# Ranking a router's experts on the chip, and giving the three smallest ranks 64 token slots instead of 96

## The chip, the cores and the metric

The kernel runs on one core of one Trainium2 chip. Its time is the device time of one execution in microseconds (us), and the time that counts is the median of the runs shown. A profiled execution of the same kernel, with a span from the first to the last instruction, is where all rows below come from.

## The reference

A decoder trunk of two layers runs on 256 tokens of width 1024 in float32. The change touches only the last stage, the expert layer of the second layer:

```python
logits = (h @ w_router + b_router).astype(jnp.float32)
top_val, top_idx = lax.top_k(logits, TOP_K)          # TOP_K = 2 of N_EXPERTS = 8
top_w = jax.nn.softmax(top_val, axis=-1)
...
for e in range(N_EXPERTS):
    out = out + gates[..., e:e + 1] * swiglu(h, wg[e], wu[e], wd[e])
```

Each token goes to two experts of eight, so there are 512 pairs of token and expert. An expert has three weight matrices of 1024 by 3584 in float32, which is 44.04 MB; the eight have 352.3 MB. With the inputs used here the reference's router gives experts 0 to 7 56, 59, 48, 73, 67, 64, 63 and 82 tokens.

## The kernel before

After attention, the recurrent mixer and the dense layer, `moe` runs the router and then the experts 0 to 7 one after the other. For each expert a one-hot matrix of token slots (`oh`, 96 slots) gathers the tokens into `g` with matmuls (`gather`), and a second one-hot matrix with the gates in it (`ohT`, made in `way_back`) brings the results back (`scatter`).

The array of TensorE is used with the tokens as the stationary operand, 32 slots at a time, and the weights as the moving one. Four such matmuls, on four groups of 32 columns of the array, take four different stretches of a weight tile. 96 slots are TG = 3 such groups of tokens, so each weight tile is streamed through TensorE three times. An expert's hidden width is cut into two parts (`PARTS`): part 0 has 16 tiles of 1 MB for gate and up (`up`, L1355) and 8 tiles of 1 MB for down (`down`, L1389), part 1 has 16 tiles of 0.75 MB and 6 of 1 MB. So an expert has 46 weight tiles. The order on TensorE is up of (expert, part), then down of the part before it, transposes of the hidden values (`hidden`), after part 0 `gather` and `way_back` of the next expert, and after the down of part 1 `scatter`.

The weight tiles come in this order of use through a ring of 15 buffers of 1 MB (`rawt` 3, `rawy` 1, `raw` 5, `rawx` 6). SyncE (SP) issues every load (L1203). It takes them in program order, so that a load waits until the tile that had its buffer 15 tiles earlier has been used, and all later loads wait behind it.

When more than 96 tokens fall on one expert, `over` is above zero and a branch at the end runs all experts again for the tokens left out. `noi`, `no` and `Go` count them. On TensorE the one matmul for that count (`pn`, L1470) stands ahead of the first `up`.

Of the kernel before, what the change touches and what calls it, by code (L numbers as in the profile page):

```python
# [21 lines left out]
P = 128  # L22
# [83 lines left out]
def tile_trunk(ctx: ExitStack, tc: tile.TileContext, a, out, fo, mo):  # L106
# [1049 lines left out]
    def moe(l, mix):  # L1156
# [6 lines left out]
        PARTS = ((0, 512), (4 * 512, 384))  # L1163
        TG, CAP = 3, 96

        def sources():

            def ups(e, s):
                c0, n = PARTS[s]
                for nm in ("w_exp_gate", "w_exp_up"):  # L1170
                    for k in range(KD):
                        yield a[nm][0, e, k * P:(k + 1) * P, c0:c0 + 4 * n].rearrange("(k p) n -> p k n", p=P)

            def downs(e, s):
                c0, n = PARTS[s]
                for r0 in range(c0, c0 + 4 * n, 2 * P):
                    yield a["w_exp_down"][0, e, r0:r0 + 2 * P, :].rearrange("(k p) n -> p k n", p=P)
# [138 lines left out]
        def gather(e):  # L1316

            oh = ep.tile([P, 2, CAP], F32, name="oh", tag="oh", bufs=1)
            for i in range(2):
                sel_ = nc.vector.tensor_scalar(oh[:, i, :], C["iota"][:, :CAP], slot_of[:, i, e:e + 1], None, op0=OP.is_equal)  # L1320
            g = gs[e] = ep.tile([P, KD, CAP], F32, name="g", tag="g", bufs=2)
            for k0 in range(0, KD, 4):
                ps = bank()[:, :4 * CAP].rearrange("p (k n) -> p k n", k=4)
                for k in range(4):
                    ks = slice((k0 + k) * P, (k0 + k + 1) * P)
                    for i in range(2):
                        nc.tensor.matmul(ps[:, k, :], xn[:, i, ks], oh[:, i, :], start=i == 0, stop=i == 1)
                for k in range(4):
                    c = k0 + k
                    affine(k0 // 4, g[:, c, :], ps[:, k, :], am[:, c:c + 1], sh[:, c:c + 1])  # L1330
            return sel_

        def way_back(e):

            ohT = st[e] = ep.tile([P, TG, S], F32, name="ohT", tag="ohT", bufs=2)
            pt = [bank("pt").rearrange("p (t n) -> p t n", t=2) for _ in range(2)]
            for i in range(2):
                oh = ep.tile([P, TG, 4, 32], F32, name="ohg", tag="ohg", bufs=2)
                nc.vector.tensor_scalar(oh, C["iota"][:, :CAP].rearrange("p (t n) -> p t n", t=TG)[:, :, None, :].to_broadcast([P, TG, 4, 32]),
                                        slot_of[:, i, e:e + 1], G[:, i, e:e + 1], op0=OP.is_equal, op1=OP.mult)  # L1340
# [3 lines left out]
            nc.vector.tensor_copy(ohT[:, 2, :], pt[1][:, 0, :])  # L1344
# [15 lines left out]
        def product_of(s, pss):  # L1360
            n, out = PARTS[s][1], []
            for t in range(TG):
# [6 lines left out]
        def hidden(s, sgs):  # L1369
# [3 lines left out]
            for t in range(TG):  # L1373
# [6 lines left out]
        def down(s, hid, acc):  # L1380

            nb = PARTS[s][1] // P
            for m in range(4 * nb):
# [3 lines left out]
                for t in range(TG):  # L1387
# [4 lines left out]
        def scatter(e, acc):  # L1392
            ohT, end = st.pop(e), e == NE - 1
            y = ep.tile([P, TG, 256], F32, name="y", tag="y", bufs=1)
            if end:
                nc.vector.tensor_tensor(y[:, 0:2, :], acc[0], gq[0][:, None, :].to_broadcast([P, 2, 256]), op=OP.mult)
                nc.vector.tensor_tensor(y[:, 2, :], acc[1], gq[0], op=OP.mult)
            else:
                nc.scalar.copy(y[:, 0:2, :], acc[0])
                nc.vector.tensor_copy(y[:, 2, :], acc[1])  # L1400
# [3 lines left out]
            for ts in ([0], [1]) if end else ([0, 1],):  # L1404
                sc = [bank("sc")[:, :256 * len(ts)].rearrange("p (i n) -> p i n", i=len(ts)) for _ in range(4)]
                for i in ts:
                    for t in range(TG):
                        for q in range(4):
                            r = slice(32 * q, 32 * q + 32)
                            nc.tensor.matmul(sc[q][:, i - ts[0], :], ohT[r, t, i * P:(i + 1) * P], y[r, t, :],  # L1410
                                             start=t == 0 and i == ts[0], stop=t == TG - 1, skip_group_check=True)
# [45 lines left out]
        gates, gf, gq, y = [], [], [], []  # L1457
        after = gather(0)
        G, t8 = small("G"), small("t8")
# [4 lines left out]
        Go = small("Go")  # L1464
        behind(nc.vector.tensor_scalar(Go, slot_of, float(CAP) + 0.5, None, op0=OP.is_ge), after)
# [8 lines left out]
        def accumulators():  # L1474
            both, one = bank("acc").rearrange("p (t n) -> p t n", t=2), psp.tile([P, 256], F32, name="acc2", tag="ada", bufs=1)
            return (both, one), [both[:, 0, :], both[:, 1, :], one]

        accs, prev = None, None
        for e, s in [(e, s) for e in range(NE) for s in range(2)] + [(None, None)]:
# [4 lines left out]
            if prev:  # L1484
                pe, ps_, hid = prev
                if ps_ == 0:
                    accs = accumulators()
                down(ps_, hid, accs[1])
# [118 lines left out]
```

## Time and profile before

| | |
|---|---|
| median of 3 runs | 1632.04 us (1624.58 to 1632.18) |
| profiled execution, its own time | 1637.66 us |
| its span | 1635.8 us |
| TensorE busy (PE) | 1559.9 us, 95% |
| TensorE weight loads (PEld) | 965.8 us, 59% |
| VectorE (DVE), ScalarE (ACT), GpSimd (POOL) | 569.0, 350.8 and 139.9 us |
| read from HBM | 472.92 MB |

PE is TensorE's matmuls, PEld its loads of stationary operands, DVE VectorE, ACT ScalarE, POOL GpSimd, SPq SyncE's queue of instructions. In a row of a timeline, a bracket gives the idle time just before and what ended it. A float32 matmul of the program is two MATMUL records in the trace, so that the 192 of an `up` are 384 records.

### The profile page before, as it was taken

The numbers are of one execution on the slowest core, as the hardware profiler recorded it, in microseconds if no ns is written. First come the engines' busy times: TensorE is split into PE (matmuls) and PEld (weight loads), VectorE is DVE, ScalarE is ACT, GpSimd is POOL, SyncE is SP. The second block draws the span as 40 slices with busy tenths as digits, with TensorE's granted clock in tenths as the row PEclk, the third lists the DMA queues.
The fourth block names the chain that finished last, engine by engine and source line by source line (L and its number), as shares of the span: only waits on it lengthen the run. The fifth ranks groups of instructions, "written<-read, shape, count | busy, mean of one in ns | idle before, by whom it ended". The sixth has DMA issues, their size and how long they took to land. (4 is left out here: it accounts for less than half of the span.)

```text
span 1635.8 us, 40608 instructions
## 1 busy us (share of the span) xinstructions
PE 1559.9 (95%) x18452; PEld 965.8 (59%) x18452; DVE 569.0 (35%) x1076; ACT 350.8 (21%) x721; POOL 139.9 (9%) x188
## 2 busy tenths in 40 slices
PE   5988999999898999999999999999999999999996
PEld 1976779999797678545355354354354454444444
DVE  2699777755569867310020010010010020110101
ACT  2723335444472323210010010010010010000001
POOL 1225100000145211000000000000000000000010
PEclk9999998999999799999999999999999999999998
DMA  9746347745463555789979979989979989989890
GB/s 319 252 169 226 136 138 274 257 169 176 141 198 130 212 178 200 290 270 415 414 291 417 414 294 417 414 294 418 411 296 417 404 302 417 393 318 416 349 378 31
DMA packets 114604, 476.65 MB, mean 291 GB/s; under 512 B 14735, under 2 KB 23707, under 8 KB 91900
## 3 DMA queue, kind: packets, MB, share of 16 engines
q1 hardware_dynamic: 111932, 469.96, 75.3%
q0 software_dynamic: 2496, 4.05, 0.9%
q8 instruction: 146, 2.39, 0.6%
q14 instruction: 30, 0.25, 0.0%
HBM read 472.92 MB, written 1.05 MB: 290 GB/s over the span
## 5 line engine op out<-in xcount | busy, mean ns | idle before, releaser
L1355 PE MATMUL up<-rawx,g 128*32 128x512 f32 (+1 forms) x2424 | 233.3, 542 | 0.0
L1365 DVE TENSOR_TENSOR sg<-sg,up 128x512 f32<-128x512 f32 (+1 forms) x48 | 29.8, 621 | 541.3 <-PE up L1355 539.8
L1355 PE MATMUL up<-raw,g 128*32 128x384 f32 (+1 forms) x2040 | 194.8, 536 | 0.0
L1355 PEld LDWEIGHTS up<-rawx,g 128*32 128x32 f32 x2424 | 78.3, 110 | 148.4 <-issue 145.2
L1355 PEld LDWEIGHTS up<-raw,g 128*32 128x32 f32 x2040 | 65.2, 110 | 125.0 <-issue 115.6
L1355 PE MATMUL up<-rawt,g 128*32 128x512 f32 (+1 forms) x1272 | 124.0, 540 | 0.0
L1389 PE MATMUL acc<-rawx,hid 128*32 128x256 f32 x2064 | 113.6, 379 | 0.0
L189 DVE TENSOR_TENSOR wlo<-raw,whi 128x512 fp32r<-128x512 f32 x140 | 96.9, 730 | 31.2 <-PE ps L169 18.1
L1389 PE MATMUL acc<-raw,hid 128*32 128x256 f32 x1872 | 103.2, 379 | 0.0
L1389 PEld LDWEIGHTS acc<-rawx,hid 128*32 128x32 f32 x2064 | 67.1, 110 | 46.2 <-issue 2.8
L187 ACT CAST whi<-raw 128x512 fp32r<-128x512 f32 x140 | 80.2, 623 | 58.9 <-PE ps L169 27.9
L169 PE MATMUL ps<-hh,whi 128*128 128x256 f32 x352 | 88.3, 288 | 1.8 <-ACT hh L187 1.8
L169 PE MATMUL ps<-hl,whi 128*128 128x256 f32 x352 | 88.3, 288 | 0.1
L169 PE MATMUL pp<-hh,whi 128*128 128x256 f32 x296 | 80.3, 306 | 6.3 <-ACT hh L187 3.7
L1355 PEld LDWEIGHTS up<-rawt,g 128*32 128x32 f32 x1272 | 40.7, 110 | 77.1 <-issue 69.5
L1389 PEld LDWEIGHTS acc<-raw,hid 128*32 128x32 f32 x1872 | 60.8, 110 | 41.2 <-PE up L1355 1.0
L1364 ACT ACTIVATE sg<-up 128x512 f32<-128x512 f32 (+1 forms) x48 | 26.1, 544 | 263.0 <-PE up L1355 263.0
L1428 POOL TENSOR_TENSOR fa<-fa,gate 128x512 f32<-128x512 f32 x4 | 5.1, 1281 | 886.1 <-ACT gate L272 886.1
L1377 ACT COPY hid<-pt 128x512 f32<-128x512 f32 (+1 forms) x32 | 17.0, 532 | 295.5 <-PE pt L1376 294.5
L169 PE MATMUL pp<-hl,whi 128*128 128x256 f32 x296 | 77.0, 294 | 0.5 <-DVE hl L189 0.2
L244 DVE SCALAR_TENSOR_TENSOR raw<-raw,ccol 128x1024 f32<-128x1024 f32 x56 | 75.0, 1359 | 0.1
L169 PEld LDWEIGHTS ps<-hh,whi 128*128 128x128 f32 x352 | 68.9, 196 | 3.7 <-ACT hh L187 2.2
(431 smaller groups left out, 2246.2 us busy)
## 6 DMA issues: line engine op xcount, KB each, us to landing
rawx<-in_w_exp_down_dram SPq DMA_DIRECT2D x43, 1024.0 KB, 11.4
raw<-in_w_ada_dram SPq DMA_DIRECT2D x40, 1024.0 KB, 6.0
raw<-in_w_exp_down_dram SPq DMA_DIRECT2D x39, 1024.0 KB, 9.9
rawx<-in_w_exp_up_dram SPq DMA_DIRECT2D x38, 1024.0 KB, 15.8
rawt<-in_w_exp_gate_dram SPq DMA_DIRECT2D x23, 1024.0 KB, 14.2
raw<-in_w_exp_gate_dram SPq DMA_DIRECT2D x30, 768.0 KB, 12.2
rawt<-in_w_exp_down_dram SPq DMA_DIRECT2D x22, 1024.0 KB, 14.3
raw<-in_w_exp_up_dram SPq DMA_DIRECT2D x21, 1024.0 KB, 16.3
```

Source lines behind the costliest of these rows:

```text
L169: nc.tensor.matmul(ps, w if left else x, x if left else w, start=start, stop=stop)
L187: c = nc.scalar.copy(hi, src)
L189: v = nc.vector.tensor_sub(lo, src, hi.bitcast(F32))
L244: nc.vector.scalar_tensor_tensor(acc[:, gs], raw[:, gs], ccol[:, k:k + 1], acc[:, gs], op0=OP.mult, op1=OP.add)
L1355: nc.tensor.matmul(ps[t][32 * j:32 * j + 32, :n], g[:, k, 32 * t:32 * t + 32], raw[:, j * n:(j + 1) * n], start=k == 0, stop=k == KD - 1)
L1364: nc.scalar.activation(sg, pss[0][t][:, :n], AF.Silu)
L1365: nc.vector.tensor_mul(sg, sg, pss[1][t][:, :n])
L1377: (nc.vector.tensor_copy if t == 1 else nc.scalar.copy)(hid[:, t, :nb].rearrange("p b n -> p (b n)"), pt[:, :nb * P])
L1389: nc.tensor.matmul(acc[t][32 * q:32 * q + 32, :], hid[:, t, b, 32 * j:32 * j + 32], raw[:, m % 2, 256 * q:256 * q + 256], start=s == 0 and ...
L1428: nc.gpsimd.tensor_mul(fa[:, i, cs], fa[:, i, cs], gates[n])
```

## The change

The number of tokens of each expert is computed on the chip (`pc`), and the experts are ranked by it: expert 0 always has rank 0, the others are ranks 1 to 7 from the most tokens to the fewest. The program takes the ranks in the fixed order 0, 1, 5, 2, 3, 6, 4, 7. Ranks 0 to 4 have 96 slots as before (three groups of 32), ranks 5, 6 and 7 have 64 (two groups): gather, up, transposes, down and scatter of these run for two groups. The weights' addresses of all but the first expert come from registers of SyncE, loaded from `num`. The slots and gates are put in the order of ranks with masks (`slotr`, `Gr`), and the count of tokens that find no slot uses 64 or 96 by rank. The rest of the kernel is as it was; `downs`, `way_back`, `product_of`, `hidden`, `scatter` and `accumulators` get the number of groups in the same way as the functions shown.

```diff
+        RANKS = (0, 1, 5, 2, 3, 6, 4, 7)
+        BIG = 4
+        groups = [3 if r <= BIG else 2 for r in RANKS]
         TG, CAP = 3, 96
+        which = [0]
         def sources():
+            def at(e):
+                return bass.ds(which[e], 1) if e else slice(0, 1)
...
-                        yield a[nm][0, e, k * P:(k + 1) * P, c0:c0 + 4 * n].rearrange("(k p) n -> p k n", p=P)
+                        yield a[nm][0, at(e), k * P:(k + 1) * P, c0:c0 + 4 * n].rearrange("o (k p) n -> p (o k) n", p=P)
...
         def gather(e):
-            oh = ep.tile([P, 2, CAP], F32, name="oh", tag="oh", bufs=1)
+            cap, r, slots = 32 * groups[e], RANKS[e], (ranked if e else by)[0]
+            oh = ep.tile([P, 2, CAP], F32, name="oh", tag="oh", bufs=1)[:, :, :cap]
...
         def up(e, s):
-            n, g, pss = PARTS[s][1], gs[e], []
+            n, g, pss, T = PARTS[s][1], gs[e], [], groups[e]
             for w in range(2):
-                ps = [bank("up") for _ in range(TG)]
+                ps = [bank("up") for _ in range(T)]
                 for k in range(KD):
                     raw = load()[:, 0]
-                    for t in range(TG):
+                    for t in range(T):
...
-        def down(s, hid, acc):
+        def down(s, hid, acc, T):
...
-                for t in range(TG):
+                for t in range(T):
...
         gates, gf, gq, y = [], [], [], []
+        G, t8 = small("G"), small("t8")
+        by, ranked = (slot_of, G), (small("slotr"), small("Gr"))
         after = gather(0)
...
-        Go = small("Go")
-        behind(nc.vector.tensor_scalar(Go, slot_of, float(CAP) + 0.5, None, op0=OP.is_ge), after)
+        pc = bank("pl")[:, :NE]
+        for i in range(2):
+            nc.tensor.matmul(pc, ones, sel[:, i, :], start=i == 0, stop=i == 1)
+        row = lambda t: t[:, None, :].to_broadcast([P, NE, NE])
+        col = lambda t: t[:, :, None].to_broadcast([P, NE, NE])
+        key, rank = ep.tile([P, NE], F32, name="key"), ep.tile([P, NE], F32, name="rank")
+        behind(nc.vector.tensor_scalar(rank, C["iota8"], -float(NE), 1.0e5, op0=OP.is_equal, op1=OP.mult), after)
+        nc.vector.scalar_tensor_tensor(key, pc, float(NE), C["iota8"], op0=OP.mult, op1=OP.subtract)
+        nc.vector.tensor_add(key, key, rank)
+        M, t64 = ep.tile([P, NE, NE], F32, name="M"), ep.tile([P, 2, NE, NE], F32, name="t64")
+        nc.vector.tensor_tensor(M, row(key), col(key), op=OP.is_gt)
+        nc.vector.tensor_reduce(rank, M, axis=AX.X, op=OP.add)
+
+        nc.vector.scalar_tensor_tensor(M, row(rank), -float(NE), col(C["iota8"]), op0=OP.add, op1=OP.is_equal)
+        nc.vector.tensor_tensor(t64[:, 0], M, row(C["iota8"]), op=OP.mult)
+        nc.vector.tensor_reduce(key, t64[:, 0], axis=AX.X, op=OP.add)
+        num = ep.tile([P, NE], I32, name="num")
+        nc.vector.tensor_scalar(num, key, float(NE), None, op0=OP.add)
+        _, nums = nc.values_load_multi_w_load_instructions(num[0:1, :], [mybir.EngineType.SP], min_val=0, max_val=NE - 1)
+        which += [nums[r] for r in RANKS[1:]]
+        for of, to in zip(by, ranked):
+            for i in range(2):
+                nc.vector.tensor_tensor(t64[:, i], M, row(of[:, i, :]), op=OP.mult)
+            nc.vector.tensor_reduce(to, t64, axis=AX.X, op=OP.add)
+
+        Go, caps = small("Go"), ep.tile([P, NE], F32, name="caps")
+        nc.vector.tensor_scalar(caps, rank, BIG + 0.5, 32.0, op0=OP.is_lt, op1=OP.mult)
+        nc.vector.scalar_tensor_tensor(Go, slot_of, -64.5, caps[:, None, :].to_broadcast([P, 2, NE]), op0=OP.add, op1=OP.is_ge)
         no = ep.tile([P, 1], F32, name="no")
         nc.vector.tensor_reduce(no, Go.rearrange("p i e -> p (i e)"), axis=AX.X, op=OP.add)
```


The first place is the start of the expert stage on TensorE. Before, from the last matmul of the slots (`pl`) to the first `up`; L1470 is the count of tokens without a slot:

```order
L1302 MATMUL pl<-sel,cf 128x8
L1303 MATMUL pl<-sel,cf 128x8
L1304 MATMUL pl<-sel,cf 128x8
L1327 MATMUL ps<-oh,xn 128x96 x16
L1470 MATMUL pl<-no,cf 128x1
L1355 MATMUL up<-rawt,g 32x512 x36
```

and now, where L1482 is `pc` and L1512 is that same count:

```order
L1312 MATMUL pl<-sel,cf 128x8
L1313 MATMUL pl<-sel,cf 128x8
L1314 MATMUL pl<-sel,cf 128x8
L1338 MATMUL ps<-oh,xn 128x96 x16
L1482 MATMUL pl<-sel,cf 128x8 x2
L1512 MATMUL pl<-no,cf 128x1
L1368 MATMUL up<-rawt,g 32x512 x36
```

`pc` has come in, and the count still stands ahead of the first `up`; it reads `no`, which VectorE makes.

On VectorE, what stands around the sum `no` for that count before (it is the L1467 row):

```order
L1465 TENSOR_SCALAR Go<-slot 128x16
L1462 TENSOR_TENSOR G<-G,t_7499 128x16 [waits DVE_49]
L1467 TENSOR_REDUCE no<-Go 128x1 [waits DVE_49]
L1339 TENSOR_SCALAR ohg<-cf,slot,G 128x384 [waits DVE_49]
L1468 TENSOR_TENSOR Go<-Go,G 128x16 [waits DVE_49]
L1339 TENSOR_SCALAR ohg<-cf,slot,G 128x384
L366 TENSOR_SCALAR g<-ps,am,modT_91 128x96 [waits PE_49]
L366 TENSOR_SCALAR g<-ps,am,modT_91 128x96 x3
```

and now, from the second row of the ranking on (the `g` rows and the first ranking row, L1487, which reads `pc`, stand just ahead; `no` is the L1509 row, `num` the L1497 row):

```order
L1488 TENSOR_TENSOR key<-key,rank 128x8 [waits DVE_49]
L1490 TENSOR_TENSOR M<-key 128x64 [waits DVE_49]
L1491 TENSOR_REDUCE rank<-M 128x8 [waits DVE_49]
L1493 SCALAR_TENSOR_TENSOR M<-rank,cf 128x64 [waits DVE_49]
L1506 TENSOR_SCALAR caps<-rank 128x8
L1494 TENSOR_TENSOR t_7514<-M,cf 128x64 [waits DVE_49]
L1502 TENSOR_TENSOR t_7514<-M,slot 128x64
L1495 TENSOR_REDUCE key<-t_7514 128x8 [waits DVE_49]
L1507 SCALAR_TENSOR_TENSOR Go<-slot,caps 128x16
L1497 TENSOR_SCALAR num<-key 128x8 [waits DVE_49]
L1502 TENSOR_TENSOR t_7514<-M,slot 128x64
L1509 TENSOR_REDUCE no<-Go 128x1 [waits DVE_49]
```

`no` stood ahead of the first `g`; now it stands behind `g` and behind the ranking, with `num` two rows ahead of it.

The second place is SyncE at the same time. Before, loads of the first expert's weights, the last of `up` in part 0 and the first of `gate` in part 1:

```order
L1203 DMA raw<-in_w_exp_up_dram 128x2048
L1203 DMA rawx<-in_w_exp_up_dram 128x2048 x6
L1203 DMA rawt<-in_w_exp_up_dram 128x2048
L1203 DMA rawt<-in_w_exp_gate_dram 128x1536 x2
L1203 DMA rawy<-in_w_exp_gate_dram 128x1536
```

and now:

```order
L1213 DMA raw<-in_w_exp_up_dram 128x2048
L1213 DMA rawx<-in_w_exp_up_dram 128x2048 x2
L1498 TENSOR_LOAD num
L1498 ISA x16
L1213 DMA rawx<-in_w_exp_up_dram 128x2048 x4
L1213 DMA rawt<-in_w_exp_up_dram 128x2048
L1213 DMA rawt<-in_w_exp_gate_dram 128x1536 x2
```

The load of the eight numbers into registers, and 16 register instructions on them, stand ahead of the last four of the six `rawx` loads. From the next expert on, a register instruction also stands ahead of each load.

The third place is TensorE in the first expert with 64 slots, its part 0. Before (an expert with 96 slots at the same place):

```order
L1376 MATMUL pt<-cf,sg 128x128 x9
L1355 MATMUL up<-rawx,g 32x512 x48
L1355 MATMUL up<-rawt,g 32x512 x36
L1355 MATMUL up<-rawy,g 32x512 x12
L1355 MATMUL up<-raw,g 32x512 x60
L1355 MATMUL up<-rawx,g 32x512 x36
L1389 MATMUL acc<-rawx,hid 32x256 x8
L1389 MATMUL acc_9020<-rawx,hid 32x256 x4
```

and now:

```order
L1389 MATMUL pt<-cf,sg 128x128 x9
L1368 MATMUL up<-rawx,g 32x512 x32
L1368 MATMUL up<-rawt,g 32x512 x24
L1368 MATMUL up<-rawy,g 32x512 x8
L1368 MATMUL up<-raw,g 32x512 x40
L1368 MATMUL up<-rawx,g 32x512 x24
L1402 MATMUL acc<-rawx,hid 32x256 x8
L1402 MATMUL acc_9116<-rawx,hid 32x256 x4
```

Each weight tile has 8 matmuls where it had 12; the down rows that follow are of the expert before, with 96 slots.

## Rows read from the trace of the kernel before

**Rows 1.** Page, the span in 40 slices (40.9 us each).

```profile
DMA  9746347745463555789979979989979989989890
GB/s 319 252 169 226 136 138 274 257 169 176 141 198 130 212 178 200 290 270 415 414 291 417 414 294 417 414 294 418 411 296 417 404 302 417 393 318 416 349 378 31
```

**Rows 2.** Windows: engines' busy time, TensorE clock, DMA share, GB/s, over one expert.

```profile
core 0: us, PE busy (x) PEld busy (x) DVE busy (x) ACT busy (x) POOL busy (x), PEclk, DMA share, GB/s
934.00:1051.00 117.00, 117.00 (x1539) 54.84 (x1535) 11.05 (x22) 7.96 (x16) 0.00 (x0) 1.00 0.94 373
```

**Rows 3.** SyncE's waits, 700 to 1600 us: total us, times, longest.

```profile
SPq L1203 <- PE up L1355: 519.8, 246, 10.3
```

**Rows 4.** Timeline of TensorE over one expert's period: start us, us, what.

```profile
961.52 2.33 PE L1355 MATMUL up<-rawy,g 128*32 128x384 f32 x24
...
1014.66 7.93 PE L1355 MATMUL up<-rawx,g 128*32 128x512 f32 x72
...
1055.88 5.36 PE L1389 MATMUL acc<-rawx,hid 128*32 128x256 f32 x96
...
1072.90 3.71 PE L1327 MATMUL ps<-oh,xn 128*128 128x96 f32 x32
...
1077.20 2.87 PE L1410 MATMUL sc<-y,ohT 32*128 32x256 f32 x48
1080.00 5.23 PE L1355 MATMUL up<-raw,g 128*32 128x384 f32 x60
```

**Rows 5.** Windows inside the expert stage, columns as in rows 2.

```profile
685.00:720.00 35.00, 35.00 (x330) 11.45 (x319) 2.73 (x5) 2.55 (x5) 0.00 (x0) 1.00 0.95 315
...
760.00:785.00 25.00, 25.00 (x389) 12.95 (x381) 0.56 (x1) 0.96 (x2) 0.00 (x0) 1.00 1.01 416
785.00:810.00 25.00, 25.00 (x240) 7.62 (x236) 0.00 (x0) 1.79 (x3) 0.00 (x0) 1.00 1.02 413
...
840.00:846.00 6.00, 6.00 (x87) 3.48 (x89) 4.12 (x8) 1.68 (x5) 0.00 (x0) 1.00 0.01 3
```

**Rows 6.** Timeline of TensorE at the stage's start.

```profile
676.86 0.31 PE L1470 MATMUL pl<-no,cf 128*128 128x1 f32 x2
677.10 7.93 PE L1355 MATMUL up<-rawt,g 128*32 128x512 f32 x72
```

**Rows 7.** Timeline of VectorE at the stage's start.

```profile
664.48 0.26 DVE L1258 TENSOR_REDUCE ws<-wams 128x8 f32<-128x64 f32 x1
...
673.57 0.16 DVE L1467 TENSOR_REDUCE no<-Go 128x1 f32<-128x16 f32 x1
...
675.28 1.24 DVE L366 TENSOR_SCALAR g<-ps,am,modT 128x96 f32<-128x96 f32 x4 [0.25 <-PE ps L1327]
```

**Rows 8.** Timelines of SyncE (its DMA issues), at the stage's start and later.

```profile
662.69 3.27 SPq L1203 DMA_DIRECT2D rawx<-in_w_exp_up_dram  x6
...
845.44 0.33 SPq L1203 DMA_DIRECT2D rawt<-in_w_exp_up_dram  x1
```

**Rows 9.** SyncE's instructions by line: count, ns min/median/max, first and last start.

```profile
L1501 SPq TENSOR_LOAD <-noi x1: 485/485/485, 835.1 to 835.1; - x1
L1501 SPq FUSED_REGOPS  x1: 186/186/186, 835.6 to 835.6; - x1
...
L1203 SPq DMA_DIRECT2D raw<-in_w_exp_gate_dram x49: 327/328/341, 624.0 to 1509.4; - x49
```

**Rows 10.** Timeline of TensorE after an idle stretch.

```profile
101.28 1.07 PE L716 MATMUL ps<-Xd,LT 32*32 32x32 f32 x64 [3.54 <-DVE Xd L729]
```

**Rows 11.** Windows around that stretch and in the first stage.

```profile
20.00:30.00 10.00, 5.82 (x28) 0.60 (x24) 2.33 (x6) 2.56 (x8) 1.59 (x3) 1.00 1.02 408
100.00:104.00 4.00, 2.72 (x72) 2.69 (x73) 3.97 (x9) 0.37 (x1) 0.00 (x0) 0.52 0.00 0
104.00:108.00 4.00, 4.00 (x86) 3.87 (x88) 1.59 (x4) 0.48 (x2) 0.00 (x0) 0.63 0.39 92
```

**Rows 12.** Timeline of TensorE, its last row.

```profile
1620.25 3.70 PE L1410 MATMUL sc<-y,ohT 32*128 32x256 f32 x48 [0.38 <-DVE y L1396]
```

More of the change, by code (lines that the diff above doesn't have):

```diff
@@ L1329, in gather @@
                     c = k0 + k
-                    affine(k0 // 4, g[:, c, :], ps[:, k, :], am[:, c:c + 1], sh[:, c:c + 1])
+                    affine(k0 // 4, g[:, c, :cap], ps[:, k, :], am[:, c:c + 1], sh[:, c:c + 1])
             return sel_
@@ L1335, in way_back @@
             ohT = st[e] = ep.tile([P, TG, S], F32, name="ohT", tag="ohT", bufs=2)
[L1336 removed]
+            T, r, (slots, gs_) = groups[e], RANKS[e], ranked if e else by
+            pt = [bank("pt").rearrange("p (t n) -> p t n", t=2) for _ in range(T - 1)]
             for i in range(2):
[L1338 to L1341 removed]
+                oh = ep.tile([P, TG, 4, 32], F32, name="ohg", tag="ohg", bufs=2)[:, :T]
+                nc.vector.tensor_scalar(oh, C["iota"][:, :32 * T].rearrange("p (t n) -> p t n", t=T)[:, :, None, :].to_broadcast([P, T, 4, 32]),
+                                        slots[:, i, r:r + 1], gs_[:, i, r:r + 1], op0=OP.is_equal, op1=OP.mult)
+                for t in range(T):
                     nc.tensor.transpose(pt[t // 2][:, t % 2, i * P:(i + 1) * P], oh[:, t].rearrange("p q n -> p (q n)"), ident)
             nc.scalar.copy(ohT[:, 0:2, :], pt[0])
[L1344 removed]
+            if T == 3:
+                nc.vector.tensor_copy(ohT[:, 2, :], pt[1][:, 0, :])
         def up(e, s):
[L1348 removed]
+            n, g, pss, T = PARTS[s][1], gs[e], [], groups[e]
             for w in range(2):
[L1350 removed]
+                ps = [bank("up") for _ in range(T)]
                 for k in range(KD):
                     raw = load()[:, 0]
[L1353 removed]
+                    for t in range(T):
                         for j in range(4):
@@ L1361, in product_of @@
             n, out = PARTS[s][1], []
-            for t in range(TG):
+            for t in range(len(pss[0])):
                 sg = ep.tile([P, 512], F32, name="sg", tag="sg", bufs=NSG)[:, :n]
@@ L1372, in hidden @@
             hid = ep.tile([P, TG, 4, P], F32, name="hid", tag="hid", bufs=2)
-            for t in range(TG):
+            for t in range(len(sgs)):
                 pt = bank("pt")
@@ L1386, in down @@
                 j, b = divmod(m, nb)
-                for t in range(TG):
+                for t in range(T):
                     for q in range(4):
@@ L1392, in scatter @@
         def scatter(e, acc):
-            ohT, end = st.pop(e), e == NE - 1
+            ohT, end, T = st.pop(e), e == NE - 1, groups[e]
             y = ep.tile([P, TG, 256], F32, name="y", tag="y", bufs=1)
@@ L1406, in scatter @@
                 for i in ts:
-                    for t in range(TG):
+                    for t in range(T):
                         for q in range(4):
@@ L1410, in scatter @@
                             nc.tensor.matmul(sc[q][:, i - ts[0], :], ohT[r, t, i * P:(i + 1) * P], y[r, t, :],
-                                             start=t == 0 and i == ts[0], stop=t == TG - 1, skip_group_check=True)
+                                             start=t == 0 and i == ts[0], stop=t == T - 1, skip_group_check=True)
                 for q in range(4):
@@ L1472, in moe, with accumulators @@
         nc.vector.tensor_copy(noi, pn)
-        def accumulators():
-            both, one = bank("acc").rearrange("p (t n) -> p t n", t=2), psp.tile([P, 256], F32, name="acc2", tag="ada", bufs=1)
-            return (both, one), [both[:, 0, :], both[:, 1, :], one]
+        def accumulators(T):
+            both = bank("acc").rearrange("p (t n) -> p t n", t=2)
+            one = [psp.tile([P, 256], F32, name="acc2", tag="ada", bufs=1) for _ in range(T - 2)]
+            return (both, *one), [both[:, 0, :], both[:, 1, :], *one]
         accs, prev = None, None
@@ L1486, in moe @@
                 if ps_ == 0:
-                    accs = accumulators()
-                down(ps_, hid, accs[1])
+                    accs = accumulators(groups[pe])
+                down(ps_, hid, accs[1], groups[pe])
             if e is not None:
```

13 lines of the change are left out of this document (7 added, 6 removed).

## The prediction

> **What bounds the kernel now.** I read the page's slices first. From slice 18 on, where the expert stage runs, the DMA engines go through 9, 9, 7 with 414, 414 and 294 GB/s, again and again [rows 1]. Two slices stand at what the weight stream can do and the third falls back, so something else stops the stream. Next, the windows: over one expert TensorE is busy 117.00 of 117 us at clock 1.00 (2.4 GHz), the DMA share is 0.94, VectorE has 11 us and ScalarE 8 [rows 2]. SyncE's waits name the limit: its loads wait 519.8 us for `up` to give a buffer back [rows 3]. So TensorE bounds the stage and the stream follows. It follows closely, though: one expert has 44.04 MB, at 416 GB/s 105.9 us, and TensorE's period is 1080.00 - 961.52 = 118.5 us [rows 4]. The margin is 12.6 us per expert, and the stream shows it as idle time while the ring is full: share 0.01 from 840 to 846 [rows 5].
>
> **What a small expert saves on TensorE.** All work from 961.52 to 1072.90 (up, down, transposes, of both parts) goes by groups of 32 slots, 111.38 us, and so does scatter, 1077.20 to 1080.00, 2.80 us [rows 4]. Two groups of three cost two thirds: (111.38 + 2.80) / 3 = 38.1 us less, about 80 us per small expert. Does the time really go by groups? A 1 MB tile takes 41.22 / 16 = 2.58 us [rows 4] for 24 records of 512 columns, and weight loads are busy 54.84 of 117 us [rows 2], so the columns set the pace and not the loads; the bounds are a third and nothing, and I take the third. Gather and way back, 4.3 us [rows 4], I count as unchanged. Three small experts: 3 x 38.1 = 114.2 us.
>
> **What the start costs.** The count of tokens without a slot is the last matmul ahead of the first `up`, at 676.86 [rows 6]. Its input `no` was made at 673.57, ahead of VectorE's share of `g` [rows 7]. Now `no` comes behind `g` (until 676.5), behind `pc` on TensorE (about 677.2) and behind thirteen small VectorE steps. Each takes 0.16 (16 elements) to 0.26 us (64 elements) [rows 7]: 2.1 to 3.4 us, I take 2.6. `up` then starts near 680.2 instead of 677.1, 3.1 us late, behind about 2.7 us of idle TensorE.
>
> That wait has a second price. After an idle stretch of 3.54 us TensorE went on at 101.28 [rows 10], and the granted clock was 0.52 and 0.63 in the two windows up to 108 [rows 11], that is about 6 us at 1.2 GHz, in which it did 3 us of work. I add 3.1 (bounds 0 and 6). Start: 6.2 us in all, 2 to 10.
>
> SyncE is held too. It issued six `rawx` loads from 662.69 [rows 8]; now four of them stand behind the load of `num`, ready near 679.5. The register load costs 0.485 us for one word [rows 9], so 0.5 to 3.9 for eight; then eight fused register steps of 0.19, 1.5 us. The four loads are issued near 683 to 685 instead of 664. That costs nothing: they are tiles 12 to 15, tile 12 is used 11 x 2.58 us behind the first `up`, at 709, and four tiles take 10 us. The lost stream time comes back, since from 685 to 720 the stream ran at only 315 GB/s [rows 5], waiting for buffers. Without that cover it would be 10 us or more. The later loads have one register step of 0.19 us beside an issue of 0.33 [rows 9]; buffers come free every 1.3 us at the fastest (a 0.75 MB tile of a small expert, 2.58 x 0.75 x 2/3), so SyncE keeps up.
>
> **Where the stall goes.** A small expert needs 80.4 us of TensorE but 105.9 us of stream: 25.5 us come out of the ring. A ring of 15 tiles is 15/46 of an expert, at most 34.5 us of stream. So the first small expert drains it nearly without a wait; two large ones give back 2 x 12.6 = 25.2 us, less than was taken; the second small one drains it again, one large one gives back 12.6, and the third runs dry. Hence the ring never gets full again after the first drain, and the stream never idles: from there the time is the stream's. The account: the last idle stretch of that kind ends near 846 now, with the issue at 845.44 of the 78th tile [rows 8], the last one of `up` of the second expert; it moves by the start to 852.2. The 77 tiles before it are 46 of the first expert (44.04 MB), 16 of 1 MB and 15 of 0.75 MB: 72.6 MB. That leaves 279.7 MB. With loads queued the stream ran at 416 and, with the 0.75 MB loads among them, 413 GB/s [rows 5]; at 414.5 it is 674.8 us, and the last tile lands at 1527.0. From landing to use no row shows a price, 0 to 2 us, I take 1. Then its matmuls (2.58 x 2/3 = 1.7), and the tail: before, down ended at 1620.25 - 0.38 = 1619.9 [rows 12] and the span at 1635.8, so 15.9 us, less a third of the 3.70 of scatter: 14.7. Sum 1544.4 against 1635.8 of span, 91.4 us less. The profiled execution took 1637.66, 5.6 above the median of the runs; the same difference from 1632.04 gives **1541 us**. TensorE alone would allow 114.2 - 6.2 = 108.0 us less, so about 17 us of waits for weights lie in the last small expert and just ahead of it, and TensorE's own small waits, as for new places of the transposes, mostly hide in them.
>
> **The rivals.**
> *TensorE stays the bound* (chance 0.08): the stream does better than 420 GB/s, or waits fall elsewhere. 1632.0 - 108.0 = 1524. Against it: no window shows more than 416.
>
> *The ring gives nothing* (0.08): each small expert takes the stream's 105.9 us, so that the gain is 3 x 12.6 - 6.2 = 31.6, 1600 us. For it: the DMA share of 0.94 [rows 2]. Against it: the full ring between 840 and 846.
>
> *The stream is slower with addresses from registers, or under full demand for long* (0.07). It decides at 279.7 MB / (674.8 + 91.4) = 365 GB/s: below that the kernel is slower than before. No row shows a load with a register's address; for it speaks the window of 315 GB/s at a share of 0.95 [rows 5], which as a lasting rate would give 888 us for the 674.8, 1754. Against it: in that window one 0.79 MB load was asked for per 2.58 us, which is 305 GB/s, and queued loads of the same size ran at 413.
> By the Trainium skill (DMA: Bandwidth & Descriptors, Bandwidth) loads from HBM are held to about 358 GB/s per core when both cores of the pair stream. By that rate the 279.7 MB would take 781 us and the kernel about 1647, slower than before. The trace disagrees for this one core: 416 GB/s over 25 us [rows 5].
>
> *TensorE falls to half clock in its waits for weights* (0.04). The last small expert would take 160 us instead of 80 plus 17 of waits: 63 more, 1604. Against it: from 20 to 30 us TensorE, fed by 1 MB loads, was busy 5.82 of 10 us at clock 1.00 [rows 11]; the waits here are under 1 us per tile.
> The Trainium skill (TensorE: Matmul & The Clock Gate, HAM oscillation) tells of a kernel that falls to the lower clock in the wait for each K-tile; the trace shows a fall behind 3.54 us, and none in that first stage.
>
> *The branch for tokens without a slot runs* (0.01): ranks 5 to 7 have 63, 59 and 48 tokens by the reference, under 64. All weights once more, at least 352.3 / 0.416 = 847 us, about 2390.
>
> **How the numbers follow.** The forecast has 0.72: 1541, on its own 1532 to 1556 (start 2 to 10 us, stream 410 to 417 GB/s, which is -4 to +7, landing 0 to 2). The range reaches down to TensorE's bound and up towards the rivals at 1600, 1520 to 1575; left out are those two, the slow stream and the branch, 0.20. About 0.5% (8 us) is what a measurement of this kernel can tell from no change. Forecast, TensorE's bound, ring and clock rivals are all faster, 0.92, of which I take 0.02 off to "same" for prices that no row shows; 0.01 of the slow stream would end within 0.5% too. So faster 0.90, same 0.03, slower 0.07.
>
> **What would show it.** In the changed profile: `up` tiles of small experts at 1.72 us; the stream at a share of 1.0 from 852 to its end near 1527 with no slice of 294 between; TensorE busy under 100% only in the last 120 us or so, with waits for DMA of under 1 us per tile; a gap of about 3 us ahead of the first `up` and a clock of 0.5 behind it; four `rawx` loads issued near 683. I am wrong if the stream idles after 860, if queued loads run below 405 GB/s, if small tiles take 2.58 us, or if the clock falls in the last expert.

## The result, and the profile after

The changed kernel takes 1553.54 us (median of 4 runs, 1551.70 to 1557.65), the kernel before 1631.89 us in the same comparison (4 runs, 1624.58 to 1632.18): ratio 0.9534, 95% interval 0.9501 to 0.9566. It is faster by 78.4 us; 1541 us was predicted, with 1520 to 1575 as the range. The profiled execution has a span of 1551.6 us, 84.2 less than before; 91.4 less was predicted.

The page's slices first (38.8 us each); they answer to [rows 1].

```profile
PE   5988998999989899999999999999999999999885
PEclk9999999999989798999999999999999999999998
DMA  9836526844545454468997999999999999999994
GB/s 321 279 116 245 184 98 242 330 188 151 181 139 178 173 209 168 149 281 329 416 414 294 415 414 412 418 413 412 418 412 388 415 413 413 415 413 417 414 411 186
```

From slice 18 on the expert stage runs. The DMA row has one 7, with 294 GB/s, where before every third slice was like that, and a small dent to 388 nine slices on; PE stands at 8 tenths in the two slices ahead of the last. Windows over the stream, with the columns of [rows 2], put numbers to it:

```profile
820.00:860.00 40.00, 40.00 (x576) 22.86 (x569) 6.31 (x14) 5.12 (x11) 0.00 (x0) 1.00 0.80 297
845.00:1150.00 305.00, 303.89 (x3912) 138.04 (x3904) 24.87 (x49) 18.59 (x37) 0.00 (x0) 1.00 1.02 412
1150.00:1190.00 40.00, 40.00 (x524) 20.49 (x520) 5.61 (x13) 4.53 (x10) 0.00 (x0) 1.00 0.98 386
1190.00:1517.50 327.50, 314.62 (x4136) 143.24 (x4128) 26.67 (x51) 19.82 (x40) 9.99 (x8) 1.00 1.02 414
1517.50:1535.00 17.50, 13.24 (x224) 6.62 (x220) 0.00 (x0) 0.00 (x0) 0.00 (x0) 1.00 0.60 238
845.00:1535.00 690.00, 671.76 (x8776) 308.38 (x8772) 57.15 (x113) 42.93 (x87) 9.99 (x8) 1.00 1.00 407
```

From 845 on the stream is busy to its end, and TensorE, which was 100% busy before, loses 12.9 of 327.5 us ahead of 1517.5. Its waits from 1430 us on (total us, times, longest) say what for:

```profile
PE acc L1402 <- DMA rawx<-in_w_exp_down_dram: 4.9, 5, 2.6
PE up L1368 <- DMA rawx<-in_w_exp_up_dram: 3.1, 6, 0.6
PE acc L1402 <- DMA raw<-in_w_exp_down_dram: 2.4, 4, 0.6
PE acc L1402 <- DMA rawt<-in_w_exp_down_dram: 2.0, 3, 0.7
```

These are waits for weights, as are nearly all of TensorE's waits there; between 845 and 1430 the whole list has 0.4 us of such waits. Three pieces of TensorE's timeline: the stage's start, against [rows 6], five tiles of a small expert, and the end, against [rows 12].

```profile
672.59 0.54 PE L1482 MATMUL pl<-sel,cf 128*128 128x8 f32 x4
675.39 0.35 PE L1512 MATMUL pl<-no,cf 128*128 128x1 f32 x2 [2.26 <-DVE no L1509]
675.67 7.93 PE L1368 MATMUL up<-rawt,g 128*32 128x512 f32 x72
...
908.09 8.77 PE L1368 MATMUL up<-raw,g 128*32 128x512 f32 x80
...
1531.19 1.93 PE L1402 MATMUL acc<-raw,hid 128*32 128x256 f32 x32 [0.62 <-DMA raw<-in_w_exp_down_dram]
1533.71 1.93 PE L1402 MATMUL acc<-raw,hid 128*32 128x256 f32 x32 [0.59 <-DMA raw<-in_w_exp_down_dram]
1536.46 2.83 PE L1425 MATMUL sc<-y,ohT 32*128 32x256 f32 x32 [0.81 <-DVE y L1409]
```

The first `up` comes 3.08 us behind the start of `pc` (1482), after 2.26 us of idle time. A tile of a small expert follows the one before it in 1.72 us (908.09 to 916.67 for five). At the end the tiles come every 2.5 us, 1.05 MB each, which is the pace of the stream.

The first `up` stands at 672.6 to 682.4 us in the profiles below, although TensorE's work ahead of it is the same in the kernels that rank, but for one width (64 slots of the first expert in three of them) and the place of the count (two). So the best yardstick is the time from the first `up` to the end of the span: 1635.8 - 677.10 = 958.7 us before and 1551.6 - 675.67 = 875.9 after, 82.8 less. All runs at a glance; each ratio is to the runs of the kernel before in the same comparison, and the last two columns are of the one profiled execution of each kernel:

| kernel | median us | ratio to before, 95% interval | first up | first up to end |
|---|---|---|---|---|
| before | 1631.9 | | 677.10 | 958.7 |
| changed | 1553.5 | 0.9534 [0.9501, 0.9566] | 675.67 | 875.9 |
| all_three | 1636.1 | 1.0017 [0.9993, 1.0041] | 676.39 | 958.7 |
| small_last | 1584.6 | 0.9711 [0.9678, 0.9743] | 674.95 | 905.6 |
| small_early | 1544.2 | 0.9462 [0.9432, 0.9492] | 672.59 | 865.4 |
| four_small | 1551.7 | 0.9496 [0.9463, 0.9528] | 682.42 | 874.9 |
| static | 1555.9 | 0.9518 [0.9479, 0.9557] | 677.90 | 878.1 |
| ring_11 | 1572.7 | 0.9628 [0.9588, 0.9668] | 674.33 | 892.4 |
| half_up | 1523.6 | 0.9323 [0.9283, 0.9363] | 672.84 | 848.0 |
| late_count | 1551.2 | 0.9497 [0.9449, 0.9545] | 674.59 | 876.6 |
| after_ahead | 1552.7 | 0.9499 [0.9465, 0.9532] | 679.65 | 876.3 |
| first_small | 1533.4 | 0.9400 [0.9362, 0.9438] | 674.20 | 856.0 |
| first_small_ahead | 1536.7 | 0.9397 [0.9361, 0.9433] | 681.23 | 854.7 |
| all_moves | 1527.2 | 0.9346 [0.9316, 0.9376] | 673.21 | 851.7 |

### The profile page after: what moved, and what is told of

It is laid out like the page before. It is cut to its first block, busy times and chain, and to the rows that moved or that the text cites. A ratio compares the mean times of both kernels' runs of the same rounds, so it can differ in the third digit from the quotient of the medians.

```text
span 1551.6 us, 38224 instructions
## 1 busy us (share of the span) xinstructions
PE 1457.0 (94%) x16941; PEld 911.3 (59%) x16941; DVE 564.0 (36%) x1080; ACT 343.9 (22%) x709; POOL 141.2 (9%) x188
## 3 DMA queue, kind: packets, MB, share of 16 engines
HBM read 472.92 MB, written 1.05 MB: 305 GB/s over the span
## 5 line engine op out<-in xcount | busy, mean ns | idle before, releaser
L1368 PE MATMUL up<-rawx,g 128*32 128x512 f32 (+1 forms) x2120 | 205.8, 542 | 3.5 <-DMA rawx<-in_w_exp_up_dram 3.3
L1368 PE MATMUL up<-raw,g 128*32 128x384 f32 (+1 forms) x1784 | 171.5, 537 | 1.6 <-DMA raw<-in_w_exp_up_dram 1.6
L1368 PEld LDWEIGHTS up<-rawx,g 128*32 128x32 f32 x2120 | 68.0, 110 | 135.4 <-issue 115.4
L1368 PEld LDWEIGHTS up<-raw,g 128*32 128x32 f32 x1784 | 57.5, 110 | 110.9 <-issue 100.2
L1368 PE MATMUL up<-rawt,g 128*32 128x512 f32 (+1 forms) x1120 | 109.7, 540 | 1.2 <-DMA rawt<-in_w_exp_up_dram 1.2
L189 DVE TENSOR_TENSOR wlo<-raw,whi 128x512 fp32r<-128x512 f32 x140 | 97.0, 729 | 32.4 <-PE ps L169 18.1
L1402 PE MATMUL acc<-rawx,hid 128*32 128x256 f32 x1792 | 100.2, 379 | 4.9 <-DMA rawx<-in_w_exp_down_dram 4.9
L1402 PE MATMUL acc<-raw,hid 128*32 128x256 f32 x1648 | 92.5, 380 | 2.4 <-DMA raw<-in_w_exp_down_dram 2.4
L1402 PEld LDWEIGHTS acc<-rawx,hid 128*32 128x32 f32 x1792 | 57.5, 110 | 45.7 <-issue 5.0
L1368 PEld LDWEIGHTS up<-rawt,g 128*32 128x32 f32 x1120 | 36.2, 110 | 68.7 <-issue 61.0
L1402 PEld LDWEIGHTS acc<-raw,hid 128*32 128x32 f32 x1648 | 52.5, 110 | 39.9 <-DMA raw<-in_w_exp_down_dram 4.3
```

What stands on the lines that cost most here:

```text
L189: v = nc.vector.tensor_sub(lo, src, hi.bitcast(F32))
L1402: nc.tensor.matmul(acc[t][32 * q:32 * q + 32, :], hid[:, t, b, 32 * j:32 * j + 32], raw[:, m % 2, 256 * q:256 * q + 256], start=s == 0 and ...
```

## The experiments

**The theory** is the prediction's: small experts take a third off TensorE's work, and from the last stop of the stream with a full ring the end is set by the bytes that are left. **The rivals**: TensorE stays the bound, so that the place of the small experts does not matter; the new start or the addresses from registers cost something of their own; the clock falls in the waits.

**all_three: ranking and registers, but no small expert.**

```diff
-        BIG = 4
+        BIG = 7
```

> BIG is 7, so all eight ranks keep three groups of 32 slots; the ranking, the load of num and the weights' addresses from registers stay. Nothing is left out. If the gain comes from the two-group experts alone, this is the kernel before plus what the ranking costs ahead of the first up, 2.8 us from the end of pc to the first up in the changed kernel: 1634 us, 1630 to 1638, with the stream idle again about once per expert. If addresses from registers slow the stream to less than TensorE's 118.5 us per expert (rival), it is 1645 us or more and TensorE waits for weights.

Measured: 1636.1 us, and 958.7 us from the first `up` to the end, as before to a tenth. The falls of the stream by its full ring are back in the page's GB/s:

```profile
GB/s 320 254 178 215 136 183 261 228 220 146 136 192 150 212 153 194 228 334 416 414 293 416 414 299 416 412 291 418 410 299 417 401 303 417 393 318 415 349 379 30
```

So the order of ranks and the register addresses cost nothing from the first `up` on while TensorE is the bound, and the two-group experts alone make the gain.

**small_last: the three small experts at the end.**

```diff
-        RANKS = (0, 1, 5, 2, 3, 6, 4, 7)
+        RANKS = (0, 1, 2, 3, 4, 5, 6, 7)
```

> RANKS is (0, 1, 2, 3, 4, 5, 6, 7): the same ranks, slots and instructions, but the three two-group experts come one behind the other at the end. Nothing is left out. Stream theory: while the first five experts run, TensorE is the bound and the stream stops once per expert with a full ring, the last time near 845.2 + 3 x 118.5 = 1200.7. Then 352.3 - 72.6 - 3 x 44.04 = 147.6 MB are left; at the changed kernel's own 688.3 us for 279.7 MB that is 363 us, the last tile lands at 1564, and with the 18.1 us from landing to the end the span is 1582, 30 us over the changed kernel's 1551.6. Theory of TensorE (the small experts save their third of TensorE's time wherever they stand): 1552 plus or minus 5.

**small_early: the first two one place earlier each.**

```diff
-        RANKS = (0, 1, 5, 2, 3, 6, 4, 7)
+        RANKS = (0, 5, 1, 2, 6, 3, 4, 7)
```

> RANKS is (0, 5, 1, 2, 6, 3, 4, 7): the first two-group expert is taken second instead of third, the second one fifth instead of sixth; the same ranks, slots and instructions. Nothing is left out. Stream theory: the stop of the stream with a full ring at 825 to 860 (20.17 MB moved from 800 to 860 where 413 GB/s would give 24.8, 11 us lost) goes away, and perhaps the 2.7 us lost at 1150 to 1190: 1538 to 1542 us, still with TensorE waiting in the last expert. Theory of TensorE: no change, 1552 plus or minus 5.

Measured: 905.6 us from first `up` to end for small_last, 29.6 more than the changed kernel (30 expected); 865.4 for small_early, 10.5 less (10 to 14 expected; its median of 1544.2 lies 2 us above the range given). Windows of small_last, where the ring drains, and of small_early, at the place where the changed kernel's stream stops (from 700 to 735 us small_early's own stream still does):

```profile
1290.00:1560.00 270.00, 226.62 (x2842) 95.30 (x2834) 20.95 (x41) 15.40 (x32) 10.00 (x8) 1.00 1.01 410
```

```profile
820.00:860.00 40.00, 39.92 (x579) 20.56 (x578) 6.33 (x13) 3.44 (x8) 0.00 (x0) 1.00 1.02 412
```

In small_last TensorE idles 43 of 270 us beside a stream at 410 GB/s. In small_early the stream moves 412 GB/s from 820 to 860 where the changed kernel moved 297. The instructions are the same in all three; only where the stream stops differs, and the time follows it. The rival that TensorE stays the bound is out.

**four_small: a fourth small expert, at the seventh place.**

```diff
-        BIG = 4
+        BIG = 3
```

> BIG is 3: rank 4, which has 64 tokens here and is taken seventh, gets 64 slots as well. Nothing is left out. Theory of TensorE: another third of an expert less, 33 to 38 us, 1514 to 1520. Stream theory: the last stop with a full ring stays where it is (825 to 860, and a little at 1150 to 1190), all bytes stay, so the end stays within 4 us of the changed kernel's, 1548 to 1556, and the 35 us turn up as waits of TensorE for weights in the last two experts. If waits of that length cost TensorE its clock (third theory), two experts at half clock are bound by TensorE at about 160 us each, and the time is above 1590.

Measured: 874.9 us from first `up` to end, 1.0 less than with three. A third of an expert was taken off TensorE and nothing came of it. The window from 1300 to 1540 of the changed kernel and of this one:

```profile
1300.00:1540.00 240.00, 221.44 (x2891) 98.16 (x2883) 17.33 (x33) 14.43 (x30) 9.99 (x8) 1.00 0.97 393
```

```profile
1300.00:1540.00 240.00, 195.58 (x2451) 78.13 (x2444) 13.57 (x25) 10.87 (x22) 9.99 (x8) 1.00 0.99 404
```

TensorE is busy 26 us less and idles as much longer. Its clock stays at 1.00 (2.4 GHz) through 44 us of waits, so the clock theory is out too.

**static: constant addresses of the weights.** The load of `num` into registers stays in the program, so that the four `rawx` loads are still held behind it, other than the expectation says; what the run tells of is the addresses alone.

```diff
-                return bass.ds(which[e], 1) if e else slice(0, 1)
+                return slice(which[e], which[e] + 1)
...
-        which += [nums[r] for r in RANKS[1:]]
+        which += [7, 6, 3, 4, 1, 5, 2]
```

> The weights' addresses are constants: the experts that the ranking finds for these inputs (7, 6, 3, 4, 1, 5, 2 behind expert 0) are written into the program, so that the loads wait for no register and four rawx loads are not held behind num; slots, ranks and order as in the changed kernel. Nothing is left out for these inputs. If addresses from registers cost the stream nothing, the stage from the first up to the end of the span is the changed kernel's 875.9 us, within 3, because the stream's loads stand queued 18 us ahead of landing: 1550 to 1556. If the register steps or the held loads are what kept the mean rate from 845 to 1535 at 407 instead of 414 GB/s (rival), it is 9 to 13 us less, 1540 to 1545.

Measured: 878.1 us, 2.2 more than with registers, and the mean rate from 845 to 1535 is 407 GB/s again. Of the 2.2 us, 1.65 are the clock at the start:

```profile
677.90 9.58 PE L1368 MATMUL up<-rawt,g 128*32 128x512 f32 x72
```

```profile
677.90:679.90 2.00, 2.00 (x13) 0.59 (x16) 0.98 (x6) 0.00 (x0) 0.00 (x0) 0.50 0.00 0
679.90:681.90 2.00, 2.00 (x16) 0.44 (x12) 0.00 (x0) 0.00 (x0) 0.00 (x0) 0.66 0.42 74
```

The same 72 records took 7.93 us in the changed kernel. Addresses from registers cost the stream nothing.

**ring_11: a ring of 11 buffers.**

```diff
-NRAWX = 6
+NRAWX = 2
```

> NRAWX is 2, so the ring has 11 buffers instead of 15. Nothing is left out. Stream theory: at the last stop with a full ring, near 1165, four tiles of 1.05 MB fewer are loaded, 4.19 MB at 413 GB/s or 10 us, and the end comes that much later: 886 us from the first up to the end, 1560 to 1566. If the gain is TensorE's and the ring gives what it gives at any size (rival), it stays at 1552 plus or minus 5.

Measured: 892.4 us, 16.5 more; 10 were expected. The direction holds, the size was short, because the smaller ring does not only hold four tiles less at the last stop, it also stops for longer there:

```profile
1150.00:1190.00 40.00, 40.00 (x559) 21.64 (x555) 6.31 (x14) 4.52 (x10) 0.00 (x0) 1.00 0.85 320
```

At 414 GB/s this window loses 40 x (1 - 320/414) = 9.1 us of stream, in the changed kernel 2.7. Four tiles (10.1 us) and 6.4 us make the 16.5 us. The account isn't closed, though: the half clock at this run's start cost another 1.7 us (9.63 us for the first 72 records), for which it leaves no room.

**half_up: every second load of the gate and up weights left out.**

```diff
-                    for k in range(KD):
+                    for k in range(0, KD, 2):
...
-                    raw = load()[:, 0]
+                    if k % 2 == 0:
+                        raw = load()[:, 0]
```

> Leaves out every second load of the up weights (each loaded tile is used for two neighbouring k), so that an expert has about 29 instead of 44 MB to load and the stream can't be the bound; all TensorE work stays. This gives TensorE's own time with two-group experts at ranks 5 to 7. By the third of the work in groups, 3 x 38.1 us less than the 958.7 us from first up to end before: 844.5. By what the changed kernel's trace shows without its waits for weights (875.9 less 17.4 us of waits and about 8 us in some 40 tiles that stand alone and show 0.2 us more each): 850. So 844 to 852 from first up to end, 1520 to 1530 in all. If the small experts save less on TensorE than a third (rival: weight loads set the pace), it is 860 or more.

Measured: 848.0 us from first `up` to end, with no wait for weights. All waits of TensorE for other engines or loads, from the first `up` on, are

```profile
PE sc L1426 <- DVE y L1410: 0.8, 1, 0.8
PE acc L1403 <- ACT hid L1391: 0.3, 1, 0.3
```

So three small experts take 958.7 - 848.0 = 110.7 us off TensorE, 36.9 each (a little over 37 without the half clock at this run's start), and 875.9 - 848.0 = 28 us of it are lost to the stream in the changed kernel. The listed waits do not add up to that: all the waits for weights of the changed kernel's TensorE make 16 us in 27 places. A tile behind a wait shows 1.93 instead of 1.72 us, an estimate of 5 us for the 27; what the rest is, no row here shows.

**late_count and after_ahead: the two costs of the start.** The first writes the count (`caps` to `noi`, now in a function `count`) behind the first part of `up`, the second issues the first expert's loads up to `rawx` ahead of the load of `num`.

```diff
             if (e, s) == (0, 0):
                 way_back(0)
+                Go, noi = count()
```

```diff
-            sync.dma_start(t, w)
+            last[:] = [sync.dma_start(t, w)]
...
-        _, nums = nc.values_load_multi_w_load_instructions(num[0:1, :], [mybir.EngineType.SP], min_val=0, max_val=NE - 1)
+        ahead.extend([issue() for _ in range(10)])
+        at_sp, nums = nc.values_load_multi_w_load_instructions(num[0:1, :], [mybir.EngineType.SP], min_val=0, max_val=NE - 1)
+        behind(at_sp[0], last[0])
```

> The count of tokens without a slot (caps, Go, no, pn, noi) is written behind the first part of up instead of ahead of it. Nothing is left out. If the chain from pc to no is what delays the first up, the first up follows pc within 0.6 us instead of 2.8 us, and since TensorE paces the stage until the last stop of the stream, the span is shorter by about 2.3 us: 1549 to 1553, which the time alone can't tell from no change; the rows at the start can. If VectorE's share of g or the rawt loads are late too (rival), up still starts over 1.5 us behind pc.

> The four rawx loads of the first expert, which have constant addresses, are issued ahead of the load of num instead of behind it (near 662 instead of 678). Nothing is left out. Theory (the held loads cost nothing, because the stream stops with a full ring at 825 to 860 anyway): 875.9 us plus or minus 3 from the first up to the end, 1549 to 1556. Rival (stream time lost at the start is lost for good): four loads, 10 us less, 1541 to 1545.

Measured: in late_count the first `up` follows the start of `pc` in 0.46 us instead of 3.08, and from there to the end it is 1551.2 - 674.13 = 877.1 us against 1551.6 - 672.59 = 879.0, 1.9 less. In after_ahead the six loads go out at once, and nothing comes of it: 876.3 us against 875.9. The rows are of late_count's TensorE and after_ahead's SyncE.

```profile
674.13 0.54 PE L1482 MATMUL pl<-sel,cf 128*128 128x8 f32 x4
674.59 7.93 PE L1368 MATMUL up<-rawt,g 128*32 128x512 f32 x72
```

```profile
662.40 3.43 SPq L1213 DMA_DIRECT2D rawx<-in_w_exp_up_dram  x6
```

**first_small, first_small_ahead and all_moves: a version meant to have no stops.** The first expert is small as well, and the order is changed; then the early loads come in, then the late count too. With 56 tokens the first expert fits 64 slots here; the tokens of rank 0 past 64 would go to the branch.

```diff
-        RANKS = (0, 1, 5, 2, 3, 6, 4, 7)
+        RANKS = (0, 1, 2, 5, 3, 6, 4, 7)
-        groups = [3 if r <= BIG else 2 for r in RANKS]
+        groups = [3 if 0 < r <= BIG else 2 for r in RANKS]
...
-        nc.vector.tensor_scalar(caps, rank, BIG + 0.5, 32.0, op0=OP.is_lt, op1=OP.mult)
+        nc.vector.tensor_scalar(caps, rank, 0.5, 32.0, op0=OP.is_gt, op1=OP.mult)
+        nc.vector.scalar_tensor_tensor(caps, rank, BIG + 0.5, caps, op0=OP.is_lt, op1=OP.mult)
```

> RANKS is (0, 1, 2, 5, 3, 6, 4, 7) and the first expert (56 tokens here) has 64 slots too, so that two-group experts stand first, fourth, sixth and eighth; tokens of rank 0 past 64 are counted for the branch with one more small step. Nothing is left out. Stream theory: the stops with a full ring at 720 to 735 (8.0 us lost in the changed kernel), 825 to 860 (11 us) and 1150 to 1190 (2.7 us) all go: 875.9 - 21.7 = 854 us from the first up to the end, 850 to 858, 1526 to 1534, and TensorE waits for weights in several experts. Theory of TensorE: 36.9 us less than the changed kernel for the fourth two-group expert, 839. Rival on the other side: the ring is drained by the first expert while four loads are held behind num, and TensorE's waits there are never made up: 864 or more.

> The kernel with two-group experts first, fourth, sixth and eighth, and the four rawx loads issued ahead of the load of num as well. Nothing is left out. Stream theory: no stop with a full ring is left to hide the 10 us in which the stream waits at the start, so here the early loads give 7 to 10 us: 844 to 847 us from the first up to the end, 1517 to 1523. If the held loads are free in any order (rival), it is as the kernel without them, 854.

> The same with the count of tokens without a slot written behind the first part of up. Nothing is left out. With all 15 buffers full at the start, the stream goes on when up gives the first one back, so an earlier up moves the whole chain: 2.6 us less from pc to the end, 1514 to 1520. Rival (the end is the stream's and does not depend on the first up): no change from the kernel without this edit.

Measured: first_small 856.0 us, in the range given (854 expected). first_small_ahead 854.7, only 1.3 less: a miss, 844 to 847 were expected (and 1517 to 1523 for the median, which is 1536.7). Windows of first_small and of first_small_ahead show where the 10 us went:

```profile
680.00:700.00 20.00, 20.00 (x192) 5.52 (x184) 0.00 (x0) 1.19 (x2) 0.00 (x0) 1.00 1.01 420
...
930.00:960.00 30.00, 30.00 (x388) 12.48 (x384) 1.67 (x3) 1.47 (x3) 0.00 (x0) 1.00 1.01 396
```

```profile
680.00:700.00 20.00, 19.26 (x150) 5.46 (x154) 1.71 (x12) 1.59 (x3) 0.00 (x0) 0.83 0.79 281
...
930.00:960.00 30.00, 30.00 (x382) 14.07 (x385) 4.51 (x10) 3.35 (x8) 0.00 (x0) 1.00 0.92 351
```

With the loads early the ring is full before the first `up` gives a buffer back, and it is full again at 930 to 960: at 414 GB/s the two windows lose 6.4 and 4.6 us, in first_small nothing and 1.3. The stop that I thought gone had moved, and all_moves has one near that place too (367 GB/s in the page's slice from 915 us on). In all_moves the first `up` comes sooner, and pc to end is 1524.9 - 672.71 = 852.2 us against 1535.9 - 677.60 = 858.3 in first_small_ahead: 6.1 less, where 2.6 were expected. The first 48 records take 5.36 us at clock 1.00 here and 8.24 us in first_small_ahead, where the granted clock behind the idle time was 0.50; that is 2.9 us of it. Another 3.1 are the first `up`, 0.50 us behind the start of `pc` here and 3.63 there.

all_moves is the fastest kernel that loads all weights, 1527.2 us, 7 above the range given, ratio 0.9346 [0.9316, 0.9376], clear of the changed kernel's 0.9534 [0.9501, 0.9566]. Against first_small's 0.9400 [0.9362, 0.9438] the intervals touch; there only the rows say that it is better, 851.7 against 856.0 us from the first `up` to the end, and 2.2 of these 4.3 us are the half clock at first_small's start (7.56 against 5.36 us for the first 48 records).

## Why the prediction was right, and what was off in it

**Right: the mechanism.** The stream takes over from the stop that ends at 844 (846 in the kernel before), and what it has left sets the end. Its three shifted forms (small_last, small_early, ring_11) and the fourth small expert that gave nothing bear that out; for the first two the same account gave the change to within 1 us. The small prices held as well: the chain at the start put the first `up` off by 2.6 us, of which 1.9 reached the end (late_count; 3.1 in the sum), and the held loads (after_ahead) and the register addresses (static) cost nothing.

**Mis-sized: the term of 674.8 us for 279.7 MB.** It took from 844, where the stream starts again, to about 1533.5, 689.5 us or 405.7 GB/s, below the 410 to 417 of the prediction's own range. (The expectation of small_last counts from 845.2 and has 688.3 us; with 844 and 689.5 its 30 us stay.)

```profile
842.00:844.00 2.00, 2.00 (x31) 0.80 (x27) 1.95 (x4) 0.18 (x1) 0.00 (x0) 1.00 0.03 8
844.00:846.00 2.00, 2.00 (x32) 0.84 (x28) 0.00 (x0) 0.00 (x0) 0.00 (x0) 1.00 0.64 181
```

At 1150 to 1190 the ring was nearly full once more, 2.7 us lost, against the step "the ring never gets full again after the first drain". The restart from 844 to 860 cost 2.5 us: it moved 5.6 MB, which is 13.5 us at 414 GB/s. And at the end, 1517.5 to 1535, the stream moved 4.2 MB in 16.0 us, 5.9 us more than at 414 GB/s, although SyncE's last weight load was issued by 1517.8:

```profile
1506.38 11.42 SPq L1213 DMA_DIRECT2D raw<-in_w_exp_down_dram  x4
```

Another 2.7 us are the 280.8 MB that 690 us at 407 GB/s make, 1.1 more than the weights counted: 1.1 MB came by a queue that the profile lists under instructions. With 0.8 us for 414 instead of 414.5 GB/s, these make 14.6 of the 14.7 us that 689.5 is above 674.8. While it ran, the stream did 414 GB/s, as forecast.

**Mis-sized: the start's second price, 3.1 us for the clock.** After 2.26 us of idle time the changed kernel went on at 1.00. Of the eleven kernels with that idle time (2.58 us in two of them) five show a clock of 0.50 to 0.70 in the first 2 us behind it, at a cost of about 1.4 to 2.9 us: static, ring_11, half_up, first_small, first_small_ahead. The other six show none. What TensorE did before it was the same in nine of them, the gather and `pc`, and three of these fell; the other two, first_small and first_small_ahead, gather 64 slots, and both fell. So the term was a chance and not a cost; bounds of 0 and 6 held.

**Mis-sized: TensorE's own gain and the tail.** 36.9 instead of 38.1 us per small expert, hidden behind the stream here. From the last landing to the end it was 18.1 us, with 1.7 + 14.7 = 16.4 in the sum.

**The sum.** From first `up` to end the forecast was 1544.4 - 680.2 = 864.2, measured 875.9: stream 689.5 - 675.8 = 13.7 more, tail 1.7, restart 0.6 earlier, clock 3.1 less. The first `up` then stood 4.5 us earlier than forecast, nearly all of it by the drift ahead of the stage (its gather starts at 668.97, in the kernel before at 673.24), which leaves 7.2 us of span. The other 5.3 us of the 12.5 between 1541 and 1553.5 come from the step that scaled the difference to the median: the profiled execution of before stood 5.6 us above its median, that of the changed kernel at it (1553.52 and 1553.54). That the narrower range of 1532 to 1556 held is in part luck: the stream took 13.7 us more where that range allowed for 7, and the clock that did not fall and the early start took 7.6 us off.

**The rivals.** TensorE as the bound has its price now: 28 us less than measured. No run shows a slow stream: 414 GB/s over 327.5 us. By the Trainium skill (DMA: Bandwidth & Descriptors, Bandwidth) a core whose neighbour streams too gets about 358 GB/s. At that rate, by an estimate from the page's figure, the kernel would have been slower than before. Only one core runs here, so the page's case did not arise and no run tests it; the prediction says too much when it has the trace disagree. By the Trainium skill (TensorE: Matmul & The Clock Gate, HAM oscillation) a wait for each tile of weights that is longer than the tile's work can bring the lower clock back each time; here waits mostly of 0.4 to 0.7 us per tile, shorter than the work of 1.5 to 1.9 us, went on for over 200 us in small_last and four_small at a granted clock of 1.00.

## What to carry to other kernels

When two engines run close together (118.5 us of TensorE and 105.9 us of stream per expert), a cut on the one that bounds is worth only what the other can follow: find the last moment at which the follower stood still, and count its bytes from there. The order of uneven pieces then matters as much as their size: the same instructions took 865 to 906 us by order alone, by where the follower stops; even the shortest of the three orders still has a stop (269 GB/s from 720 to 735 us in small_early). A stop that is removed may only move; look for it in the next window before its price is counted as won.

## What the runs showed that was not expected

At the end of a long stretch of streaming the DMA engines do not finish together: at 1525 to 1530 the share is about half and the tiles still come at the pace of the full stream.

```profile
1520.00:1525.00 5.00, 3.79 (x68) 2.04 (x64) 0.00 (x0) 0.00 (x0) 0.00 (x0) 1.00 0.88 351
1525.00:1530.00 5.00, 3.80 (x72) 1.81 (x68) 0.00 (x0) 0.00 (x0) 0.00 (x0) 1.00 0.53 211
1530.00:1535.00 5.00, 3.79 (x68) 1.84 (x64) 0.00 (x0) 0.00 (x0) 0.00 (x0) 1.00 0.17 66
```

The trace keeps 16 completion marks for each load, as many as there are DMA engines. Those of the last weight tile lie from 1523.2 to 1533.7 us, the last one 5.4 us behind their mean, which is nearly the 5.9 us above. From the first mark to the last it is 0.6 us for the tile that lands at 848, 7.9 at 1140, 3.9 at 1195, behind the short stop at 1150 to 1190, and 10.5 at the end. In the kernel before, whose stream stops about once per expert, it is never more than 4.5 us from 846 on. So the engines drift apart while the stream runs and are closer together behind a stop, and a stream that runs on to its end pays for the drift there. Which engines lag, and why, the marks do not tell. Nor does any run tell why the clock fell behind the same idle time in some kernels and not in others.
